# Two-layer hybrid decoder trunk: whole rows of the output projection behind the last pair of heads, and an opening of the MLP in a written-out order with two column pairs interleaved

## The chip, the cores and the metric

One core of one Trainium2 chip runs the whole program. The metric is the device time of one execution in microseconds (us). PE is TensorE, DVE is VectorE, ACT is ScalarE, POOL is GpSimd, SP is the engine that issues most of the DMAs.

## The reference, cut to what matters

Sequence 1024, width 1024, 12 mixing heads and 4 memory heads of 64, MLP width 2816, two layers.

```python
for layer in range(2):
    xn = rmsnorm(h, norm_mix[layer])
    heads = concat(mixer(xn), memory_attention(xn, mem))      # layer 0 FoX, layer 1 dilated
    h = h + merge_heads(heads) @ w_out[layer]                 # the output projection
    u = rmsnorm(h, norm_ffn[layer]) @ w_up[layer]             # 1024 -> 5632
    val, gate = split(causal_depthwise_conv3(u))
    h = h + (silu(gate) * val) @ w_down[layer]
return rmsnorm(h, norm_final)
```

## The kernel before, in words

**Number format.** Every float32 operand of a large product is split into a rounded high part and a low part, and each product is made of three matmuls: high·high, high·low, low·high (`mm3g`, L172, the matmuls on L177 to L179). A weight block is loaded by `load_w` (L107): DMA into `wraw`, cast to `whi` on ACT (L122), subtraction to `wlo` on POOL (L123). There are three `whi`/`wlo` pairs and four `wraw` buffers.

**Layout.** Activations are feature-major: eight blocks of 128 features, two halves of 512 positions. Heads are worked two at a time in six pairs. The attention loop (L808) runs 96 steps: step s issues the scores of block s, the transposes of block s-2 (L495, copied out by ACT on L496 and DVE on L497) and, for odd blocks, the product with the values of block s-3 (L800). `fold` (L499) adds the two halves of such a product and, for the last pair, writes its high and low part straight into the operand tile (L508, L509). An object `Fill` puts chunks of other PE work between these pieces, paced by a cost and a due step given to each item.

**Output projection.** A row n (128 features of h) needs eight chunks of 128 head features. Chunk 5 belongs to the last pair and is ready last. `out_part(half)` (L567) makes seven of the eight chunks for all eight rows as fill work and adds them to the residual (L582): for half 0 due by step 94, for half 1 due by step 104, so that part of half 1 is left to `fill.drain` behind the loop. `out_final` (L300) then adds the eighth chunk of all eight rows from one weight block `wol`, with the residual on L293 and the squares for the norm on L154 to L158. For half 0 it runs inside the loop at step 94, for half 1 at the start of the MLP (L1001). `norm_stages` (L134) turns the squares into a scale: a column sum on PE (L138), DVE, a power on POOL (L142), a diagonal on DVE (L144), a broadcast on PE (L148).

**MLP up-projection.** 22 column pairs j. Each is made by seven products (a Strassen-like scheme) of 4 chunks x 3 matmuls from seven operand sets TS[0] to TS[6], which are sums and differences of quarters of the normalised h. `up_x0` (L351) makes sets 0 and 1 from half 0, `up_x1` (L360) makes sets 2 to 6 from half 1: normalisation on DVE (L348), sum on DVE or POOL (L342), cast on ACT (L343), low part on DVE or POOL (L344). The weight sums of a pair come from `w_alpha` to `w_gamma` (L880 to L909), with casts on L912 and low parts on L915, from raw loads on L870. Products of one pair are combined in PSUM on DVE (L943 to L961), then convolved (`conv_a` on ACT, L971; two `conv_d` on DVE, L975), gated (L979, L983) and stored.

**What sets the order.** In attention and at the start of the MLP only PE follows the order of the code; ACT, DVE, POOL and the DMA queue are ordered by the tile scheduler. From pair 2 on (L1039) PE, ACT, DVE and POOL all follow the order of the code. Pairs 0 and 1 are made before that, largely product by product (L1004 to L1034): the products wait for `up_x1`, and pair 2 waits for PSUM banks that the convolutions of pairs 1 and 0 still read.

```python
run(out_final(l, 1, acc, lambda n: bank_of("all", ALL)))   # L1001
...
product(1, 4, 4)
up_x1(l, rb)                                               # L1012
for j, b in ((0, 0), (1, 4)):
    u21(j)
    product(j, 3, b + 1)
```

Of the kernel before, what the change touches and what calls it, by code (L numbers as in the profile page):

```python
# [29 lines left out]
def trunk(ctx, tc, a, out):  # L30
# [76 lines left out]
    def load_w(src, cols=1024):  # L107
        hi = sb.tile([P, 1024], R32, tag="whi", name="whi", bufs=3)
        lo = sb.tile([P, 1024], R32, tag="wlo", name="wlo", bufs=3)
# [190 lines left out]
    def out_final(l, half, acc, psum):  # L300
        oh, ol = O[l, half]
        c = NPAIR - 1
        hi, lo = load_w(a["wol"][l])
        for n in range(KD):
            ps = psum(n)
            mm3(ps, lambda k: cols(hi)(n), lambda k: cols(lo)(n), lambda k: oh[:, c, :], lambda k: ol[:, c, :], 1)
            residual(ps, n, half, PART[l] if half else None)
            nc.sync.dma_start(hf_scr[l][n][half], H[half](n))
            square_acc(acc, H[half](n), n == 0)
            yield n  # L310
# [6 lines left out]
    def t_tile(i):  # L317
        if i < 4:
            t = sb.tile([P, 2, 4, HT], R32, tag=("xh0", "xl0", "xh1", "xl1")[i], name=f"t{i}")
            TS[i] = lambda x, c: t[:, x, 2 * c:2 * c + 2, :]  # L320
        else:
            us = []
            for u in range(4):
                v = 4 * (i - 4) + u
                us.append((qk(f"t{i}") if v < 10 else ptt(f"t{i}", [P, T])).rearrange("p (k t) -> p k t", k=2))
            TS[i] = lambda x, c: us[2 * x + c]
        return TS[i]
# [7 lines left out]
    def t_make(i, c, a0, a1, op, e0, e1):  # L335

        t = TS[i] if i in TS else t_tile(i)
        hi, lo = t(0, c), t(1, c)
        src = a0
        if a1 is not None:  # L340
            src = (a1 if i == 5 else a0) if i > 4 else qk("tsum", F32).rearrange("p (k t) -> p k t", k=2)
            e0.tensor_tensor(src, a0, a1, op=op)  # L342
        nc.scalar.copy(hi, src)  # L343
        e1.tensor_tensor(lo, src, hi.bitcast(F32), op=ALU.subtract)  # L344
# [6 lines left out]
    def up_x0(l, rb):  # L351
        TS.clear()
        V, G = nc.vector, nc.gpsimd
        norm_in_place(l, 0, rb, range(KD))
        for c in range(2):
            t_make(0, c, quarter(0, 0, c), None, None, None, (V, G)[c])
        for c in range(2):
            t_make(1, c, quarter(1, 0, c), quarter(0, 0, c), ALU.subtract, (V, G)[c], (V, V)[c])

    def up_x1(l, rb):  # L360
        V, G = nc.vector, nc.gpsimd
        q = quarter
        norm_in_place(l, 1, rb, (0, 1, 4, 5, 2, 3, 6, 7))
        for c in range(2):
            t_make(2, c, q(0, 1, c), q(1, 1, c), ALU.subtract, V, (V, G)[c])
        for c in range(2):
            t_make(3, c, q(1, 1, c), None, None, None, (G, V)[c])
        for c in range(2):
            t_make(4, c, q(0, 0, c), q(1, 1, c), ALU.add, (V, G)[c], (V, V)[c])
        for c in range(2):  # L370
            t_make(5, c, q(0, 0, c), q(0, 1, c), ALU.add, (V, G)[c], V)
        for c in range(2):
            t_make(6, c, q(1, 0, c), q(1, 1, c), ALU.add, (V, G)[c], V)


    def attention_phase(l):
        with tc.manual_schedule(engines={mybir.EngineType.PE}):
# [189 lines left out]
            def out_part(half):  # L567
# [4 lines left out]
                else:  # L572
                    hp = [qk("hp", F32).rearrange("p (n t) -> p n t", n=2) for _ in range(4)]
                    dst = PART[l] = lambda n: hp[n // 2][:, n % 2, :]
                for n in range(KD):
                    load_h(l, n, half, dst)
                for n in range(KD):
# [7 lines left out]
            def out_last():  # L585
                acc = sqt("acc")
                for n in out_final(l, 0, acc, lambda n: psp()):
                    yield 648
                g = norm_stages(acc, psp)
                while True:  # L590
                    yield None
                    rb = next(g)
                    if rb is not None:
                        break
                up_x0(l, rb)
# [127 lines left out]
            QK, V, OP = 24 * 216, 96 * 113, 168 * 216  # L723
# [32 lines left out]
            fill.add(out_part(0), OP, 94, 83, "o0")  # L756
            fill.add(out_part(1), OP, 104, 84, "o1")
# [50 lines left out]
            for s in range(len(seq) + D + 1):  # L808
# [9 lines left out]
                if b % 2 == 1:  # L818
# [5 lines left out]
                    if s == LAST:  # L824
                        fill.need("o0")
                        while next(last, None) is not None:
                            fill.step()
# [5 lines left out]
                if s in (LAST + 2, LAST + 3):  # L833
                    next(last, None)
                fill.go(0.30 if b % 2 == 1 else 0.50)
            fill.drain()


# [4 lines left out]
    def ffn(l):  # L843
# [9 lines left out]
        sets = itertools.cycle("wpwpw")  # L853
        two = lambda t: t.rearrange("p (q n) -> p q n", q=2)

        def w_set():
            if next(sets) == "w":
                return (two(sb.tile([P, 1024], R32, tag="whi", name="ahi", bufs=3)),
                        two(sb.tile([P, 1024], R32, tag="wlo", name="alo", bufs=3)))
            return two(ptt("ahi", [P, 1024])), two(ptt("alo", [P, 1024]))  # L860
# [56 lines left out]
        def prep(j):  # L917
            w_raw(j)
            for f, eng in ((w_alpha, G), (w_beta, G), (w_delta, V), (w_gamma, G)):
# [76 lines left out]


        prep(0)
        h_tiles(1)
        acc = sqt("acc")  # L1000
        run(out_final(l, 1, acc, lambda n: bank_of("all", ALL)))  # L1001
        prep(1)
        st = norm_stages(acc, lambda: bank_of("norm", (3, 7)))
        product(0, 2, 2)  # L1004
        s_copy(0, 2)
        next(st)
        product(1, 2, 6)
        s_copy(1, 2)
        product(0, 4, 0)
        rb = next(st)  # L1010
        product(1, 4, 4)
        up_x1(l, rb)  # L1012
        for j, b in ((0, 0), (1, 4)):
            u21(j)
            product(j, 3, b + 1)
            s_copy(j, 3)
            s_diff(j)
        for j, b in ((0, 0), (1, 4)):
            product(j, 5, b + 3)
            u12(j)  # L1020
        for j, b in ((0, 0), (1, 4)):
            product(j, 1, b + 2)
            s_e(j)
            g_1(j)
            g_2(j)
        w_raw(2)
        for j, b in ((1, 4), (0, 0)):
            product(j, 6, b + 1)
            u22(j)
        for j, b in ((0, 0), (1, 4)):  # L1030
            product(j, 7, b + 2)
            u11(j)
        whole(1, 4)
        whole(0, 0)  # L1034
        for f in (w_alpha, w_beta, w_delta, w_gamma):
            o = f(2)
            cast(o)
            rest(o, G)
        with tc.manual_schedule(engines={mybir.EngineType.PE, mybir.EngineType.Activation, mybir.EngineType.DVE,  # L1039
                                         mybir.EngineType.Pool}):  # L1040
            one = itertools.cycle((4, 5, 6, 7))
            for j in range(2, FFC):
                k = j + 1
                more, back = k < FFC, j > 2
# [3 lines left out]
                if back:  # L1048
                    u11(j - 1)
                    conv_a(j - 1, 0, 0)  # L1050
                    conv_d(j - 1, 1, 1)
                s_copy(j, 2)
                product(j, 3, next(one))
                if back:
                    conv_d(j - 1, 1, 2)
                    silu(j - 1)
                    conv_d(j - 1, 0, 1)
# [3 lines left out]
                if back:  # L1061
                    conv_d(j - 1, 0, 2)
# [230 lines left out]
```

## Time and profile before

| | us |
|---|---|
| median of 3 runs | 2657.45 (2651.96 to 2662.17) |
| profiled execution, its own time | 2654.48 |
| its span | 2652.7 |
| PE busy in it | 2453.4 (92%) |
| mean granted clock of PE | 0.969 of full |

Each busy time is a share of the span; a busy PE is not always a PE at full clock, so the granted clock of a stretch is read beside it. What an engine waited for stands in brackets behind an instruction of the timeline: the idle time just before it, and the instruction that ended the wait.

### The profile page before, as it was taken

The page shows a single profiled execution, that of the slowest core. Times are in us where ns is not written, and L with a number is a line of the kernel's source. Part 1 is how long each engine was busy: PE and PEld are TensorE (multiplying, and loading weights), DVE is VectorE, ACT ScalarE, POOL GpSimd, SP SyncE. Part 2 cuts the span into 40 slices and gives each one's busy share as a digit, 9 for nine tenths or more (in the row PEclk, how much of TensorE's full clock was granted, in tenths as well). Part 3 has the DMA queues.
Part 4 walks back from the last instruction along what each step waited for, and adds up shares of the span by engine and source line. Part 5 has one row for each costly group of instructions (what it writes and reads, how often), then busy time and mean ns, then how long its engine had stood idle before and what let it go on. Part 6 is the DMA issues. An engine that isn't in the chain of part 4 may idle for free. (4 is left out here: it accounts for less than half of the span.)

```text
span 2652.7 us, 34480 instructions
## 1 busy us (share of the span) xinstructions
PE 2453.4 (92%) x12280; PEld 2044.6 (77%) x12280; DVE 1645.2 (62%) x2824; ACT 1204.8 (45%) x2189; POOL 1232.9 (46%) x764
## 2 busy tenths in 40 slices
PE   4989999987799999999998999989878999999998
PEld 3868888776588888888877888877657888887886
DVE  5667676666866666633347777775777666666322
ACT  4545555543343444443345555564434343444321
POOL 4201101344667666555543333335545667665542
PEclk9999999998899999999999999999989999999999
DMA  5122222431222222654432222244212222237432
GB/s 179 46 77 73 61 68 88 145 123 64 76 83 88 76 92 73 227 186 138 151 118 63 61 59 70 61 119 146 99 48 97 87 79 88 77 120 234 147 121 79
DMA packets 144980, 271.15 MB, mean 102 GB/s; under 512 B 18844, under 2 KB 23580, under 8 KB 144808
## 3 DMA queue, kind: packets, MB, share of 16 engines
q1 hardware_dynamic: 143944, 268.26, 31.4%
q8 instruction: 96, 1.57, 0.3%
q10 hardware_dynamic: 864, 0.69, 0.1%
q14 instruction: 76, 0.62, 0.1%
HBM read 200.67 MB, written 47.24 MB: 93 GB/s over the span
## 5 line engine op out<-in xcount | busy, mean ns | idle before, releaser
L123 POOL TENSOR_TENSOR wlo<-wraw,whi 128x512 fp32r<-128x512 f32 x354 | 468.6, 1344 | 788.0 <-ACT whi L122 693.6
L177 PE MATMUL PS<-t,ahi 128*128 128x512 f32 x1056 | 418.7, 396 | 34.7 <-ACT t L343 11.4
L178 PE MATMUL PS<-t,ahi 128*128 128x512 f32 x1056 | 416.1, 394 | 11.7 <-DVE t L344 11.7
L179 PE MATMUL PS<-t,alo 128*128 128x512 f32 x1056 | 415.7, 394 | 0.0
L177 PE MATMUL PS<-xh,whi 128*128 128x512 f32 x704 | 311.9, 443 | 29.9 <-DVE hp L582 9.6
L122 ACT CAST whi<-wraw 128x512 fp32r<-128x512 f32 x354 | 202.8, 607 | 223.9 <-issue 65.1
L178 PE MATMUL PS<-xl,whi 128*128 128x512 f32 x704 | 289.5, 411 | 9.1 <-POOL xl L289 4.5
L179 PE MATMUL PS<-xh,wlo 128*128 128x512 f32 x704 | 288.0, 409 | 4.3 <-POOL wlo L123 4.3
L177 PEld LDWEIGHTS PS<-t,ahi 128*128 128x128 f32 x1056 | 201.4, 191 | 81.5 <-issue 17.0
L971 ACT ACTIVATE cv<-PS,cw 128x1024 f32<-128x1024 f32 x88 | 106.2, 1209 | 318.6 <-DVE PS L952 311.2
L178 PEld LDWEIGHTS PS<-t,ahi 128*128 128x128 f32 x1056 | 201.4, 191 | 54.8 <-DVE t L344 12.7
L179 PEld LDWEIGHTS PS<-t,alo 128*128 128x128 f32 x1056 | 201.1, 190 | 42.5
L975 DVE SCALAR_TENSOR_TENSOR cv<-PS,cw,cv 128x1023 f32<-128x1023 f32 (+1 forms) x176 | 221.0, 1277 | 12.7 <-ACT cv L971 10.0
L915 POOL TENSOR_TENSOR alo<-araw,ahi 128x1024 fp32r<-128x1024 f32 x84 | 204.6, 2435 | 33.2 <-ACT ahi L912 33.2
L486 ACT ACTIVATE y<-y,m 128x128 f32<-128x128 f32 (+1 forms) x192 | 149.4, 778 | 117.2 <-DVE m L482 115.2
L497 DVE TENSOR_TENSOR ptl<-PS,pth 128x512 fp32r<-128x512 f32 (+3 forms) x288 | 152.4, 550 | 62.4 <-ACT pth L496 61.5
L177 PEld LDWEIGHTS PS<-xh,whi 128*128 128x128 f32 x704 | 140.4, 199 | 59.3 <-ACT xh L288 10.3
L496 ACT CAST pth<-PS 128x512 fp32r<-128x512 f32 (+3 forms) x288 | 131.2, 479 | 114.9 <-PE PS L495 113.4
L179 PEld LDWEIGHTS PS<-xh,wlo 128*128 128x128 f32 x704 | 139.4, 198 | 36.2 <-POOL wlo L123 5.2
L178 PEld LDWEIGHTS PS<-xl,whi 128*128 128x128 f32 x704 | 140.2, 199 | 32.3 <-POOL xl L289 7.8
L1106 DVE TENSOR_TENSOR g<-graw,g 128x512 fp32r<-128x512 f32 x88 | 90.8, 1063 | 107.7 <-ACT g L1105 107.7
L495 PE MATMUL PS<-ident,y 128*128 128x128 f32 x864 | 130.5, 278 | 28.3 <-DVE ptl L497 28.1
(202 smaller groups left out, 5764.6 us busy)
## 6 DMA issues: line engine op xcount, KB each, us to landing
araw<-in_wu SPq DMA_DIRECT2D x176, 256.0 KB, 3.6
wraw<-in_wd SPq DMA_DIRECT2D x168, 256.0 KB, 3.1
gscr<-cv SPq DMA_DIRECT2D x44, 512.0 KB, 2.6
graw<-gscr SPq DMA_DIRECT2D x88, 256.0 KB, 3.9
wraw<-in_wo SPq DMA_DIRECT2D x64, 256.0 KB, 3.0
wraw<-in_wq SPq DMA_DIRECT2D x56, 256.0 KB, 2.9
hfscr<-h SPq DMA_DIRECT2D x32, 256.0 KB, 2.1
h<-hfscr SPq DMA_DIRECT2D x32, 256.0 KB, 3.7
```

The costliest lines, as they stand in the source:

```text
L122: nc.scalar.copy(hi[:, w], raw[:, :n])
L123: nc.gpsimd.tensor_tensor(lo[:, w], raw[:, :n], hi[:, w].bitcast(F32), op=ALU.subtract)
L177: nc.tensor.matmul(ps, lhsT=whi(k), rhs=xhi(k), start=(first and k == 0), stop=False)
L178: nc.tensor.matmul(ps, lhsT=whi(k), rhs=xlo(k), start=False, stop=False)
L179: nc.tensor.matmul(ps, lhsT=wlo(k), rhs=xhi(k), start=False, stop=(last and k == nk - 1))
L486: nc.scalar.activation(y[:, :nk], y[:, :nk], AF.Exp, bias=m[:, npc - 1:npc], scale=-1.0, accum_out=m[:, 2:3])
L495: nc.tensor.transpose(tp[:, jj, :], y[:, j * P:(j + 1) * P], ident)
L496: nc.scalar.copy(ph, tp[:, :nj, :])
L497: nc.vector.tensor_tensor(pl, tp[:, :nj, :], ph.bitcast(F32), op=ALU.subtract)
L915: eng.tensor_tensor(o[2], o[0], o[1].bitcast(F32), op=ALU.subtract)
L971: nc.scalar.activation(t, u, AF.Identity, bias=w(3), scale=w(2))
L975: V.scalar_tensor_tensor(t[:, d:], u[:, :T - d], w(2 - d), t[:, d:], op0=ALU.mult, op1=ALU.add)
```

## The change: what it does

For half 0, `out_part` makes six partial rows in place of eight; rows 6 and 7 are made whole, with eight chunks, by the new `out_rest`, which also adds the last chunk to rows 0 to 5. For half 1 there are four partial rows, due by step 98 in place of 104, and four whole ones. The order of the whole rows ("c") and last chunks ("f") is written out, over the three score banks (half 0) or four banks (half 1). In the loop, steps 94 to 98 each take a few of them. The sum of squares runs one row late. `up_x0` and the new order of `up_x1` have all sums and low parts on DVE. The weights of the pairs alternate between the `pt` and `qk` buffers, operand sets 5 and 6 move into the `whi`, `wlo` and `tab` buffers, and the down-projection's weights move to `pt`. Pairs 0 and 1 have each product twice in a row, one for each pair, their combination is regrouped (`s_less`, `g_0`), and pair 2's products alternate with the convolutions of pairs 1 and 0. PE, ACT, DVE and POOL all follow the code's order from the half-1 rows on.

```diff
-    def load_w(src, cols=1024):
-        hi = sb.tile([P, 1024], R32, tag="whi", name="whi", bufs=3)
+    def load_w(src, cols=1024, home=None):
+        hi = home("whi", [P, 1024]) if home else sb.tile([P, 1024], R32, tag="whi", name="whi", bufs=3)
...
-    def out_final(l, half, acc, psum):
+    def out_rest(l, half, acc, psum, order):
...
+        for i, (kind, n) in enumerate(order):
+            if kind == "f":
+                wl = wl or load_w(a["wol"][l])
+                hi, lo, ks = *wl, [(NPAIR - 1, n)]
+            else:
+                hi, lo, ks = *load_w(a["wo"][l, n]), [(c, c) for c in KORD]
+            ps = psum()
...
+            residual(ps, n, half, PART[l] if half and kind == "f" else None)
             nc.sync.dma_start(hf_scr[l][n][half], H[half](n))
+            sq = acc if i == 0 else sqt("sq")
+            nc.scalar.activation(sq, H[half](n), AF.Square)
+            if late is not None:
+                nc.vector.tensor_tensor(acc, acc, late, op=ALU.add)
...
+    def t_rest(i, c):
+        nc.vector.tensor_tensor(TS[i](1, c), SUM[i, c], TS[i](0, c).bitcast(F32), op=ALU.subtract)
...
-            fill.add(out_part(0), OP, 94, 83, "o0")
-            fill.add(out_part(1), OP, 104, 84, "o1")
+            fill.add(out_part(0, 6), 6 * OP, 94, 83, "o0")
+            fill.add(out_part(1, 4), 4 * OP, 98, 84, "o1")
...
+                order = [("c", 6)] + [("f", n) for n in range(6)] + [("c", 7)]
...
-        sets = itertools.cycle("wpwpw")
+        sets = itertools.cycle([ptt] * 3 + [qk_set] * 3)
...
+        for j in range(2):
+            w_raw(j)
+            prep(j, (w_alpha, w_beta, w_delta, w_gamma)[:4 - j], G)
...
+        with tc.manual_schedule(engines=engines):
+            acc = sqt("acc")
+            run(out_rest(l, 1, acc, lambda: bank_of("fin", (0, 1, 2, 3)),
+                         [("c", 4), ("f", 0), ("f", 1), ("c", 5), ("f", 2), ("f", 3), ("c", 6), ("c", 7)]))
+            prep(1, (w_gamma,), G)
+            product(0, 2, 6)
+            s_copy(0, 2)
+            st = norm_stages(acc, lambda: bank_of("norm", (7, 5)))
+            next(st)
+            product(1, 2, 2)
+            s_copy(1, 2)
+            product(0, 4, 0)
+            rb = next(st)
+            product(1, 4, 4)
+            u21(0)
+            for c in range(2):
+                norm_in_place(l, 1, rb, (4 + 2 * c, 5 + 2 * c))
+                SUM[3, c] = q(1, 1, c)
+                t_cast(3, c)
+            t_rest(3, 0)
...
+            product(0, 5, 3)
+            product(1, 5, 7)
+            product(0, 3, 1)
+            s_copy(0, 3)
+            s_less(0)
+            product(1, 3, 6)
+            s_copy(1, 3)
+            s_less(1)
+            for c in range(2):
+                t_sum(4, c, q(0, 0, c), q(1, 1, c), ALU.add)
+                t_cast(4, c)
...
+            product(1, 7, 6)
+            product(0, 7, 2)
+            w_raw(2)
+            u22(1)
+            conv_a(1, 1, 4)
+            prep(2, (w_alpha, w_beta), G)
...
+            product(2, 2, 4)
...
+            product(2, 1, 6)
+            u22(0)
+            conv_a(0, 1, 0)
...
-                hi, lo = load_w(a["wd"][l, b0 + b])
+                hi, lo = load_w(a["wd"][l, b0 + b], home=ptt)
```

## Rows read from the trace of the kernel before

**Rows 1.** The page: span and busy time of each engine.

```profile
span 2652.7 us, 34480 instructions
PE 2453.4 (92%) x12280; PEld 2044.6 (77%) x12280; DVE 1645.2 (62%) x2824; ACT 1204.8 (45%) x2189; POOL 1232.9 (46%) x764
```

**Rows 2.** Windows: span, busy PE, PEld, DVE, ACT, POOL (instructions), granted clock, DMA.

```profile
563.10:646.00 82.90, 64.44 (x268) 48.73 (x268) 60.07 (x78) 33.96 (x55) 38.95 (x22) 0.91 0.27 96
646.00:724.20 78.20, 59.58 (x227) 46.40 (x227) 64.21 (x57) 29.28 (x32) 40.61 (x17) 0.85 0.19 64
1815.00:1861.50 46.50, 45.95 (x248) 39.17 (x247) 28.26 (x70) 25.59 (x54) 26.60 (x20) 1.00 0.36 114
1860.90:1943.50 82.60, 63.92 (x268) 48.62 (x267) 59.74 (x77) 33.88 (x53) 38.94 (x22) 0.91 0.28 97
1943.50:2021.45 77.95, 59.13 (x227) 46.01 (x227) 64.16 (x57) 29.23 (x32) 41.16 (x17) 0.86 0.18 64
2040.00:2080.00 40.00, 40.00 (x178) 33.12 (x177) 26.52 (x32) 16.20 (x18) 27.07 (x14) 1.00 0.24 88
```

**Rows 3.** Timeline of PE, layer 1, projection: start, us, [idle before <-releaser].

```profile
1863.05 0.49 PE L177 MATMUL PS<-xh,whi 128*128 128x512 f32 x1 [2.10 <-ACT xh L508]
1872.41 0.51 PE L177 MATMUL PS<-xh,whi 128*128 128x512 f32 x1 [0.39 <-DVE h L293]
1884.08 1.54 PE L495 MATMUL PS<-ident,y 128*128 128x128 f32 x6 [2.10 <-DVE ptl L497]
1917.41 0.47 PE L177 MATMUL PS<-xh,whi 128*128 128x512 f32 x1 [2.78 <-DVE hp L582]
1932.38 0.80 PE L179 MATMUL PS<-xh,wlo 128*128 128x512 f32 x1 [2.32 <-POOL wlo L123]
1943.50 0.80 PE L177 MATMUL PS<-t,ahi 128*128 128x512 f32 x1 [4.53 <-DVE h L293]
```

**Rows 4.** Timeline of PE, layer 1, opening of the MLP.

```profile
1964.70 0.80 PE L177 MATMUL PS<-t,ahi 128*128 128x512 f32 x1 [5.72 <-ACT t L343]
1971.34 0.80 PE L178 MATMUL PS<-t,ahi 128*128 128x512 f32 x1 [5.84 <-DVE t L344]
2007.34 0.77 PE L177 MATMUL PS<-t,ahi 128*128 128x512 f32 x1 [4.10 <-DVE cv L975]
```

**Rows 5.** Timeline of DVE, layer 1, around the last product with the values.

```profile
1892.16 2.87 DVE L144 TENSOR_TENSOR dg<-ident,nrs 128x512 f32<-128x512 f32 x1
1898.46 5.34 DVE L348 SCALAR_TENSOR_TENSOR h<-h,gains,PS 128x512 f32<-128x512 f32 x8
1908.08 0.69 DVE L505 TENSOR_TENSOR fold<-PS,fold 64x512 f32<-64x512 f32 x1
1914.91 1.64 DVE L509 TENSOR_TENSOR xl<-fold,xh 64x512 fp32r<-64x512 f32 x1
```

**Rows 6.** Lines L344 and L342: duration ns min/median/max.

```profile
L344 DVE TENSOR_TENSOR t<-tsum,t x10: 1209/1226/3357, 613.6 to 1981.8; 128x1024 fp32r<-128x1024 f32 x10
L342 DVE TENSOR_TENSOR tsum<-h,h x8: 2036/2838/3381, 607.9 to 1971.2; 128x1024 f32<-128x1024 f32 x8
L343 ACT CAST t<-tsum x12: 1043/1045/1057, 612.5 to 1976.9; 128x1024 fp32r<-128x1024 f32 x12
```

**Rows 7.** Timeline of POOL and ACT, layer 1.

```profile
1910.26 1.30 POOL L123 TENSOR_TENSOR wlo<-wraw,whi 128x512 fp32r<-128x512 f32 x1
1917.65 2.37 POOL L915 TENSOR_TENSOR alo<-asum,ahi 128x1024 fp32r<-128x1024 f32 x1
2014.44 0.59 ACT L935 COPY s<-PS 128x512 f32<-128x512 f32 x1 [2.08 <-PE PS L179]
2016.99 1.21 ACT L971 ACTIVATE cv<-PS,cw 128x1024 f32<-128x1024 f32 x1 [1.01 <-POOL cv L983]
```

**Rows 8.** Groups by line, DVE, two pairs of the steady loop (2060 to 2098 us).

```profile
L975 DVE SCALAR_TENSOR_TENSOR cv<-PS,cw,cv 128x1023 f32<-128x1023 f32 (+1 forms) x8 | 10.1, 1278 | 0.1
L884 DVE TENSOR_TENSOR asum<-araw 128x1024 f32<-128x1024 f32 x2 | 2.4, 1216 | 0.0
L946 DVE TENSOR_TENSOR PS<-PS,s 128x512 f32<-128x512 f32 x3 | 2.1, 700 | 6.1 <-PE PS L179 6.1
```

More of the change, by code (lines that the diff above doesn't have):

```diff
@@ L564, in mem_attn, with out_part @@
                     fill.go(.3)
-            def out_part(half):
+            def out_part(half, rows):
                 oh, ol = load_o(l, half)
@@ L586, in out_last @@
                 acc = sqt("acc")
[L587 to L592, printed above, removed]
+                order = [("c", 6)] + [("f", n) for n in range(6)] + [("c", 7)]
+                yield from out_rest(l, 0, acc, lambda: bank_of("fin", (0, 1, 2)), order)
+                for rb in norm_stages(acc, psp):
                     if rb is not None:
-                        break
-                up_x0(l, rb)
+                        up_x0(l, rb)
+                    yield
             def forget():
@@ L825, in attention_phase @@
                         fill.need("o0")
-                        while next(last, None) is not None:
-                            fill.step()
+                        next(last)
+                    elif s == LAST + 2:
+                        for _ in range(4):
+                            next(last)
+                    elif s == LAST + 4:
+                        next(last)
                     fill.go(.1)
@@ L832, in attention_phase, with qk_set @@
                     emit_t(s - D)
-                if s in (LAST + 2, LAST + 3):
-                    next(last, None)
+                if s == LAST + 1:
+                    for _ in range(3):
+                        next(last)
+                elif s == LAST + 3:
+                    next(last)
                 fill.go(0.30 if b % 2 == 1 else 0.50)
             fill.drain()
+    def qk_set(name, shape):
+        return qk(name)
     def ffn_phase(l):
@@ L852, in ffn @@
         A, R = {}, {}
-        sets = itertools.cycle("wpwpw")
+        sets = itertools.cycle([ptt] * 3 + [qk_set] * 3)
         two = lambda t: t.rearrange("p (q n) -> p q n", q=2)
         def w_set():
[L857 to L860, printed above, removed]
+            home = next(sets)
+            return two(home("ahi", [P, 1024])), two(home("alo", [P, 1024]))
         def w_raw(j):
@@ L1018, in ffn @@
[L1018 to L1038, printed above, removed]
@@ L1041, in ffn @@
             one = itertools.cycle((4, 5, 6, 7))
-            for j in range(2, FFC):
+            for j in range(3, FFC):
                 k = j + 1
-                more, back = k < FFC, j > 2
+                more = k < FFC
                 if more:
@@ L1116, in g1_tile @@
             two = lambda t: t.rearrange("p (x t) -> p x t", x=2)
-            return two(qk("g1") if k < 18 else ptt("g1", [P, T]))
+            if k < 18:
+                return two(qk("g1"))
+            return two(sb.tile([P, T], R32, tag=("whi", "wlo")[k % 2], name="g1", bufs=3))
         G1 = []
```

213 lines of the change are left out of this document (131 added, 82 removed).

## The prediction

> **What bounds the kernel now.** The page comes first: PE is busy 92% of the span and no other engine reaches two thirds [rows 1]. So time can come only from PE's idle 200 us and from the stretches in which it works at the lower of its two clocks, 1.2 instead of 2.4 GHz. Next, a table of the span in windows shows where these lie. In the steady loop of the up-projection PE is busy 40.00 of 40 us at full clock, 178 matmuls, so 0.225 us each [rows 2]. The change touches two stretches per layer. Stretch A goes from the end of the product that frees half 0 to the first MLP product; stretch B goes on to the point where pair 2 is three products in and PE runs without gaps. In layer 1, A has 82.60 - 63.92 = 18.7 us idle, and a granted clock of 0.91 over 82.6 us costs at most 0.09 x 82.6 = 7.4 us: 26 us. B has 18.8 us idle and 0.14 x 78 = 10.9 us from the clock: 30 us. Layer 0 gives 26 and 30 as well [rows 2]. That is 56 us per layer, **112 us in all, the whole pool.**
>
> Then the timeline of PE, read for its brackets, says what ended each wait. In A: the high part of the last pair's output (2.10), the residual of a last chunk (0.39, seven times alike or longer), transposes behind DVE (2.10), partial rows behind DVE (2.78), a late low part of the weights (2.32), and the bank of the last row (4.53) [rows 3]. In B: operand sets 2 and 3, of which PE waits first for a cast, then for a low part (5.72, 5.84), and a convolution that holds a bank (4.10) [rows 4]. After most of these gaps matmuls start to start take about twice as long for a few us; that is the clock's part.
>
> **The change, part by part.** The matmuls are the same in number, only their order differs, and so are the loads on SP: 16 row blocks and two last-chunk blocks per layer. So everything below is waiting.
>
> *Pace of the fill.* Ten partial rows over 14 steps (0.67 row per step by the code's arithmetic) replace a pace of 0.76. PE was busy 45.95 of 46.50 us there [rows 2]; with 0.09 x 21 x 0.225 = 0.4 us less work per step, PE either goes faster or idles 0.4 us. Bounds 0 and 4 us per layer; I take 0, since PE was the full engine.
>
> *Half 0 (steps 94 to 98).* A whole row of 24 matmuls (5.4 us) with the last pair's chunk at its end now stands where PE waited 2.10 us, so the fold is covered; three banks and other work between the last chunks remove the 0.39s. What is late next: the score banks are shared with the rows, 0.5 us (0 to 2, at most two such DVE passes). The last transposes come right before the last values product; PE waited 2.10 us for such a copy before; I take 1 (0 to 2.1). The scale needs POOL and a DVE diagonal that took 2.87 us beside POOL [rows 5]; PE has some 3 us of work meanwhile; 0.5 (0 to 2.9).
>
> *Half 1.* The first whole row now starts right behind the last values product. Its seven earlier chunks last 21 x 0.225 = 4.7 us; the fold's two DVE steps spanned 8.5 us before (1908.08 to 1916.55) because normalisation stood between them [rows 5]. The fold is now issued ahead of normalisation, so I take 1 (0 to 4). The weights' low parts on POOL, 1.30 each [rows 7], two per row, go beside six pair splits of 2.37; PE waited 2.32 once before; 1.5 (0 to 5). **DVE is what is late next.** Behind the last values product it has the fold (1.4), eight normalisations (5.34), six operations of 1024 columns at 1.21, and some 3 us of weight sums [rows 5, 6, 8]: 17 us before it adds the first whole row to the residual. PE wants that row's bank again after 0.5 + 5.4 + 1.4 + 5.4 = 12.7 us. So 5 us (0 if DVE gets to the residual between, 11 if its operations stretch as far as the 3.36 us rows). Clock loss behind these waits: 4 (2 to 7.4). Sum for A: 0.5 + 1 + 0.5 + 1 + 1.5 + 5 + 4 = 13.5 us, bounds 6 to 24 since not all happen together.
>
> *Opening (B).* I walk the written order with a product as 2.7 us, normalisation 0.67, cast 1.05, sum and low part 1.21, PSUM combination 0.61 to 0.70, convolution 1.21 and 1.28 [rows 5 to 8], zero at the norm's scale. No sum of two quarters ran below 2.04 us [rows 6], since POOL was always at work beside it; the same shape took 1.22 as a weight sum [rows 8], and here POOL has only one 512-column subtraction per pair, so I take 1.21 (up to 3.38).
> - Product (1,4) ends at 2.7. Set 3's second low part waits for six normalisations, a combination and two low parts: 7.1. Products on set 3 end 2.8 us late.
> - Set 2 is complete at 13.9; wait 2.2.
> - Set 4: its first cast stands on ACT behind the copy of product (1,3) (0.59) [rows 7], which ends at 18.5; its second low part is ready at 25.2, behind one sum for set 5; wait 5.5, the largest.
> - Sets 5 and 6 are then in time.
> - PE ends these products at 40.3. Pair 2's products wait for convolutions in banks 4 to 7 and 0 to 3, with the raw weights of pair 2 landing just before: 1.6 + 3.0 + 1.1 + 2.6.
>
> Sum 18.8 us of waits; clock behind the three larger ones 5 (2 to 10): 24 us, bounds 17 to 35. The gaps of 5.72, 5.84 and 4.10 shrink to one of 5.5 and several below 3. What hides the rest is the other pair's product, 2.7 us each; without it each wait would be longer by that.
>
> *Weights and down-projection buffers.* Six sets in place of five, three pairs for the down weights as before: 0, hidden by a PE that is full there [rows 2]; the price if this fails is the fourth rival.
>
> **Sum.** Per layer (26 - 13.5) + (30 - 24) = 18.5 us, twice 37. The profiled execution took 2654.5 (span 2652.7), 3.0 below the median of 2657.45. So 2617.5 for such an execution and **2620 for the median.**
>
> **Rivals.**
> - *The waits all but close*: DVE takes residuals between its other work, casts come earlier than my walk has them. A 7, B 18: 2 x (19 + 12) = 62, 2595. For: every wait of rows 3 and 4 is addressed by a reordering. Against: DVE was already busy 64 of 78 us in B [rows 2].
> - *DVE takes PE's place.* All sums and low parts move from DVE and POOL to DVE. The low parts took 1.21 us at least and 3.36 at most [rows 6], the long ones beside POOL. At 1.8 us each my walk gives 28.7 us of waits, 35 with the clock, and A 18.5: 2 x (7.5 - 5) = 5 us gained, 2652. For: POOL has 20 us of splits behind the last values product. Against: in the opening POOL is nearly empty. The Trainium skill, page "SBUF — State Buffer", section "Who interferes with whom", speaks against this change: a DVE instruction with two SBUF inputs and a GpSimd instruction that reads SBUF use one shared read interface, and the one that is issued second is blocked until the first ends. By that rule A comes out as in this rival and B as in my walk, 2 x (7.5 + 6) = 27 us gained, 2630; the spread of rows 6 agrees with it.
> - *The change doesn't do what it says*: POOL gets the splits of pairs 0 and 1 ahead of the first whole row's weights. Those splits wait for buffers that the last values product still reads and for raw loads that wait for the first splits: 1 + 6 us of POOL, 5 us of loading, then 5 us of casts and sums and 7 us of POOL, two low parts: the first whole row starts some 26 us late. A 34 with DVE's backlog gone: 2 x (-8 + 6), 2661. Against: the same kind of splits was interleaved with weights before, one of each within 8 us [rows 7].
> - *Slower: the steady loop loses its cover.* Sets 5 and 6 sit in the `whi`, `wlo` and two of three `tab` buffers, so the next pair's weight sum has one buffer, and DVE stands still in its written order if that is not free. Price: 38 pairs; from 1 us per pair the change is lost, at 1.5 us it is 2620 + 57 = 2677. Against: sum, cast and low part take 1.2 + 1.05 + 2.4 = 4.7 us of a pair's 84 x 0.225 = 18.9 [rows 2, 6 to 8]; it decides only if they end 14 us later than that.
>
> **How the numbers follow.** Forecast 0.59, waits closed 0.15, DVE 0.12, POOL's order 0.06, steady loop 0.08. A measurement of this kernel can tell about 0.5%, 13 us, from no change. Faster by more: 0.59 + 0.15 = 0.74; within: 0.12 + 0.06 = 0.18; slower: 0.08. The bounds of A and B put the forecast's own case at 2600 to 2643; the range reaches to 2586, which takes in most of the closed case, and to 2655, which takes in the DVE case, and leaves out POOL's order, the steady loop and the tail below, under 0.2.
>
> **What would show it.** Right: in A no brackets behind the last pair's high part nor runs of 0.39 behind residuals, the granted clock of A and B above 0.93, a bracket of about 5 us behind DVE at the fifth or sixth piece of half 1, and one in the opening at set 4. Wrong: brackets over 2 us behind `wlo` at the first whole row (POOL's order), DVE without idle time through B with low parts over 1.8 us (DVE's case), or any PE gap per pair in the steady loop.

## The result, and the profile after

The kernel after takes **2687.56 us** (median, 2681.34 to 2691.83) beside 2654.70 for the kernel before: ratio **1.0118, interval 1.0085 to 1.0151**. It is slower by 1.2%, where 2620 was forecast. The profiled execution took 2691.83, the longest of its four, with a span of 2689.8. One execution in the experiments below, of the early operand alone on the kernel after, took 4091.9 us at a granted clock of 0.556 and is left out of its median.

The page, span and busy engines, beside [rows 1]:

```profile
span 2689.8 us, 34462 instructions
PE 2465.0 (92%) x12280; PEld 2044.5 (76%) x12280; DVE 1605.5 (60%) x2822; ACT 1206.6 (45%) x2189; POOL 1186.6 (44%) x754
```

PE's work is the same. The windows (columns as in [rows 2]) show where it stands: the end of attention, the rows of half 1 in layers 0 and 1, and the steady loop.

```profile
540.00:565.00 25.00, 20.14 (x98) 15.06 (x97) 11.27 (x30) 12.50 (x25) 15.81 (x13) 1.00 0.39 128
565.00:600.00 35.00, 34.73 (x185) 29.17 (x184) 23.39 (x40) 15.80 (x29) 11.75 (x8) 1.00 0.27 98
600.00:640.00 40.00, 16.68 (x41) 10.45 (x41) 27.00 (x24) 15.00 (x21) 22.83 (x12) 0.63 0.32 107
1920.00:1960.00 40.00, 19.17 (x49) 13.10 (x50) 26.40 (x24) 13.45 (x18) 19.79 (x11) 0.62 0.33 112
2080.00:2120.00 40.00, 40.00 (x178) 33.14 (x177) 27.14 (x33) 17.15 (x19) 25.17 (x12) 1.00 0.22 79
```

The first two windows of the kernel before:

```profile
540.00:565.00 25.00, 23.08 (x125) 19.19 (x123) 13.97 (x33) 14.05 (x29) 17.57 (x13) 1.00 0.45 147
565.00:600.00 35.00, 29.04 (x124) 21.12 (x125) 26.13 (x38) 15.29 (x28) 14.25 (x10) 0.90 0.31 110
```

In layer 0, half 0 behind the last pair went as planned: 34.73 of 35 us busy, against 29.04. Layer 1 kept one wait there, for the bank of a row whose residual was late:

```profile
1900.43 0.79 PE L177 MATMUL PS<-xh,whi 128*128 128x512 f32 x1 [2.10 <-DVE h L293]
```

Before half 0's rows 3 us are lost, and then comes the loss itself: of the 40 us behind the last product with the values PE works 17 to 19, at 0.62 to 0.63 of full clock. The timeline of PE says for what, from 600 us on, beside [rows 3]; layer 1 has the same six waits, each within 0.3 us:

```profile
611.26 0.80 PE L177 MATMUL PS<-xh,whi 128*128 128x512 f32 x1 [10.39 <-ACT whi L122]
629.20 0.79 PE L177 MATMUL PS<-xh,whi 128*128 128x512 f32 x1 [9.29 <-ACT whi L122]
631.83 0.79 PE L179 MATMUL PS<-xh,wlo 128*128 128x512 f32 x1 [1.41 <-POOL wlo L123]
635.85 0.80 PE L177 MATMUL PS<-xh,whi 128*128 128x512 f32 x1 [1.95 <-ACT whi L122]
648.56 0.80 PE L177 MATMUL PS<-xh,whi 128*128 128x512 f32 x1 [3.05 <-ACT whi L122]
659.32 0.50 PE L177 MATMUL PS<-xh,whi 128*128 128x512 f32 x1 [2.01 <-ACT whi L122]
```

In half 1 nothing of [rows 3] is left; in its place PE waits mostly for **casts of weights**. The queues show why each cast is late. First SP's issues:

```profile
596.49 9.08 SPq L879 DMA_DIRECT2D araw<-in_wu  x4
605.62 0.90 SPq L121 DMA_DIRECT2D wraw<-in_wo  x2
```

The first whole row's weights are issued behind four loads for pair 1 (L879), whose buffers POOL frees (SP waits 11.8 us for POOL's low parts there); their cast follows 5 us later. Then ACT:

```profile
610.59 1.13 ACT L122 CAST whi<-wraw 128x512 fp32r<-128x512 f32 x2
...
627.06 1.04 ACT L921 CAST ahi<-araw 128x1024 fp32r<-128x1024 f32 x1 [5.77 <-DVE araw L907]
628.01 0.63 ACT L317 ACTIVATE acc<-h 128x512 f32<-128x512 f32 x1
628.54 1.12 ACT L122 CAST whi<-wraw 128x512 fp32r<-128x512 f32 x2
633.38 0.63 ACT L317 ACTIVATE sq<-h 128x512 f32<-128x512 f32 x1 [3.71 <-DVE h L293]
634.66 0.63 ACT L317 ACTIVATE sq<-h 128x512 f32<-128x512 f32 x1 [0.65 <-DVE h L293]
635.20 0.60 ACT L122 CAST whi<-wraw 128x512 fp32r<-128x512 f32 x1
```

The second of these casts, at 628.54, is that of the last-chunk block. The loop of `out_rest` writes each block's cast (L122) behind the square of the row before it (L317). From half 1 on ACT follows the code, so a block is cast only when PE has made the row before, DVE has added it and ACT has squared it: a round trip at each block. The first trip is long because DVE gets to the residual only at 626.95, behind pair 1's weight sums.

In the opening of layer 0 the waits are short, beside [rows 4]:

```profile
681.47 0.50 PE L178 MATMUL PS<-t,ahi 128*128 128x512 f32 x1 [0.87 <-DVE t L360]
691.10 0.50 PE L178 MATMUL PS<-t,ahi 128*128 128x512 f32 x1 [0.76 <-DVE t L360]
696.87 0.49 PE L177 MATMUL PS<-t,adia 128*128 128x512 f32 x1 [1.62 <-ACT t L357]
736.34 0.76 PE L177 MATMUL PS<-t,ahi 128*128 128x512 f32 x1 [2.36 <-DVE cv L983]
```

**The balance by landmarks.** From half 0's first projection matmul to the first MLP product it is 150.3 and 152.1 us before, 169.9 and 173.6 after: 41 lost. From there to the first down-projection matmul it is 448.2 and 447.9 before, 440.6 twice after: 15 gained. The other 11 of the 37 us between the two spans lie thinly, 2 ahead of the first projection, 6 between the layers, 3 at the end; they were not traced to a cause.

### The profile page after: what moved, and what is told of

The parts are those of the page before. It is cut to its first block, busy times and chain, and to the rows that moved or that the text cites. A ratio compares the mean times of both kernels' runs of the same rounds, so it can differ in the third digit from the quotient of the medians.

```text
span 2689.8 us, 34462 instructions
## 1 busy us (share of the span) xinstructions
PE 2465.0 (92%) x12280; PEld 2044.5 (76%) x12280; DVE 1605.5 (60%) x2822; ACT 1206.6 (45%) x2189; POOL 1186.6 (44%) x754
## 5 line engine op out<-in xcount | busy, mean ns | idle before, releaser
L123 POOL TENSOR_TENSOR wlo<-wraw,whi 128x512 fp32r<-128x512 f32 x354 | 462.6, 1327 | 826.3 <-ACT whi L122 712.9
L122 ACT CAST whi<-wraw 128x512 fp32r<-128x512 f32 x354 | 202.9, 607 | 225.5 <-issue 54.7
L924 POOL TENSOR_TENSOR alo<-araw,ahi 128x1024 fp32r<-128x1024 f32 x88 | 212.4, 2414 | 7.8 <-ACT ahi L921 7.8
L178 PEld LDWEIGHTS PS<-xl,whi 128*128 128x128 f32 x704 | 142.3, 202 | 47.4 <-POOL xl L289 21.7
L293 DVE TENSOR_TENSOR h<-h,PS 128x512 f32<-128x512 f32 x56 | 37.7, 684 | 230.2 <-PE PS L1283 141.1
```

What stands on the lines that cost most here:

```text
L122: nc.scalar.copy(hi[:, w], raw[:, :n])
L123: nc.gpsimd.tensor_tensor(lo[:, w], raw[:, :n], hi[:, w].bitcast(F32), op=ALU.subtract)
L178: nc.tensor.matmul(ps, lhsT=whi(k), rhs=xlo(k), start=False, stop=False)
L924: eng.tensor_tensor(o[2], o[0], o[1].bitcast(F32), op=ALU.subtract)
```

## The experiments

All times are medians. The kernel before was measured anew beside each of the four groups of runs (2657.58, 2656.69, 2655.84 and 2654.20), and the ratios are to that. Differences of medians across groups carry up to 3 us of this spread.

### The casts, the loads, the written order

Casts ahead: the weight blocks are loaded and cast ahead of the squares, in the same order as they are used.

```diff
         for i, (kind, n) in enumerate(order):
+            for key in (ahead or {}).get(i, ()):
+                weights(key)
...
-                         [("c", 4), ("f", 0), ...]))
+                         [("c", 4), ("f", 0), ...], ahead={0: (4, "l", 5), 3: (6,), 6: (7,)}))
```

> The changed kernel, with one thing different: in the whole rows of half 1 each weight block is loaded and cast one row earlier in the written order (the first three blocks ahead of the first row, the fourth ahead of the second whole row, the fifth ahead of the third). Theory 'squares': in the written order ACT casts the next row's weights only after the square of the row before, and that waits for PE and DVE. Then the brackets behind the cast and the low part of the weights after the first (9.3, 1.4, 2.0, 3.1, 2.0, 0.6 us in layer 0) fall below 1 us each, some 18 us and 4 us of clock per layer, and the first of 10.4 us stays or changes by less than 4: about 2645. Theory 'loads': the raw loads stand on SP behind pair 1's raw loads and behind stores, so the casts only find another thing to wait for; the brackets keep their sum within 5 us per layer and end on a DMA: 2675 to 2690.

Loads first: the first whole row's block and the last-chunk block are loaded and cast ahead of the splits of pairs 0 and 1.

```diff
+        pre = {k: load_w(a["wol"][l] if k == "l" else a["wo"][l, k]) for k in (4, "l")}
         for j in range(2):
             w_raw(j)
```

> The changed kernel, with the loads and casts of the first whole row's weights and of the last-chunk block of half 1 issued ahead of the splits of pairs 0 and 1; nothing else is moved. Theory 'loads': the first bracket (10.4 us) falls to under 3, the second (9.3 us) stays within 3 us of that or falls with it since its load is ahead too, the later ones (1.4 to 3.1) stay: 10 to 20 us and some clock per layer, 2640 to 2665. Theory 'squares' alone: the first bracket stays, since the first row's cast has no square of this half before it; 2680 to 2690.

Rows unwritten: `out_rest` of half 1 stands outside the block in which ACT, DVE and POOL follow the code.

```diff
+        run(out_rest(l, 1, acc, ...))
         with tc.manual_schedule(engines=engines):
-            run(out_rest(l, 1, acc, ...))
```

> The changed kernel, with the rows of half 1 outside the written order: PE keeps it, but ACT, DVE and POOL are ordered by the scheduler there, as in the kernel before. Theory 'squares': the scheduler puts casts ahead of squares, so the brackets after the first go as in the run with casts ahead, about 2645. Theory 'loads': as with casts ahead, 2675 to 2690. If the whole rows as such were the cost (more row weights behind the last pair), nothing of it changes: 2685.

Measured: casts ahead 2649.42, ratio 0.9971 [0.9959, 0.9982]; rows unwritten 2646.79, 0.9973 [0.9963, 0.9983]; loads first 2673.14, 1.0072 [1.0054, 1.0089]. The first two come out near what the theory of the squares gave; loads first lies between its two theories. PE with the casts ahead:

```profile
611.09 0.79 PE L177 MATMUL PS<-xh,whi 128*128 128x512 f32 x1 [10.40 <-ACT whi L122]
621.76 0.50 PE L177 MATMUL PS<-xh,whi 128*128 128x512 f32 x1 [1.26 <-ACT whi L122]
...
631.37 0.80 PE L179 MATMUL PS<-xh,wlo 128*128 128x512 f32 x1 [4.75 <-POOL wlo L123]
```

PE with the loads first:

```profile
607.54 0.50 PE L177 MATMUL PS<-xh,whi 128*128 128x512 f32 x1 [1.17 <-ACT xh L519]
609.04 0.50 PE L178 MATMUL PS<-xl,whi 128*128 128x512 f32 x1 [1.01 <-DVE xl L520]
625.42 0.79 PE L177 MATMUL PS<-xh,whi 128*128 128x512 f32 x1 [14.27 <-ACT whi L122]
```

The two edits take away different waits. The written order on ACT is worth 38 us: with the casts ahead the 9.29 falls to 1.26 and the waits behind later casts are gone, though a new wait of 4.75 us for a low part on POOL stands in their place. The edit moves a block's load together with its cast. It matters little whether the blocks are written ahead or left to the scheduler. The loads are worth 14 us alone; the 10.4 falls to the fold's 2.2, but the next cast then waits 14.27 behind the square.

Both together:

> Both parts together: the loads of the first whole row and of the last-chunk block are issued ahead of the splits of pairs 0 and 1, and each later block's load and cast is written ahead of the squares before it. Theory (two queues in written order, SP and ACT, each holds the weights back): the wait of 10.4 us at the first whole row shrinks to the fold's 2 us as it did with the loads moved alone, and the waits behind casts at rows 5, 6 and 7 stay gone as they did with the casts moved alone; row 5's load is still behind pair 1's, so up to 5 us may stay there. 2 x 6 us below the 2649 of the casts alone: 2637, between 2630 and 2643, under both the kernel before and every version so far. Rival (DVE's residuals, my prediction's 5 us, are next in line and take over): gaps behind 'DVE h' of 5 us or more appear in the rows, and the time stays at 2645 to 2650. Rival (the two parts cover the same wait): 2649, no further gain.

> The first two loads ahead of the splits, and the rows of half 1 outside the written order, so that the scheduler places their casts, squares, residuals and low parts. Theory: the same as loads and casts together, 2636 (2628 to 2642); the 10.4 us at the first whole row falls to 2 to 3 us. Rival (the scheduler puts the pair splits' casts ahead of row 5's whatever the loads' order): a gap of 8 to 14 us behind ACT whi at row 5, and 2646.

Measured: **2637.63**, 0.9928 [0.9913, 0.9943]; unwritten 2640.15, 0.9943 [0.9927, 0.9960]. Both times lie in the expected ranges. But the wait that the rival named is there too, 9.81 us with loads and casts together and 13.04 with the rows unwritten. PE with loads and casts together:

```profile
627.15 0.80 PE L177 MATMUL PS<-xh,whi 128*128 128x512 f32 x1 [9.81 <-DVE h L293]
```

It stands at the fifth piece, where the first row's bank is wanted again. DVE in the same run:

```profile
620.93 5.57 DVE L914 TENSOR_TENSOR araw<-araw 128x512 f32<-128x512 f32 x2
626.42 0.67 DVE L293 TENSOR_TENSOR h<-h,PS 128x512 f32<-128x512 f32 x1
```

Pair 1 behind the rows: in the code all its loads, casts and splits, with the casts ahead.

```diff
-        for j in range(2):
-            w_raw(j)
-            prep(j, (w_alpha, w_beta, w_delta, w_gamma)[:4 - j], G)
+        w_raw(0)
+        prep(0, (w_alpha, w_beta, w_delta, w_gamma), G)
...
-            prep(1, (w_gamma,), G)
+            w_raw(1)
+            prep(1, (w_alpha, w_beta, w_delta, w_gamma), G)
```

> Casts written ahead, and all loads and splits of pair 1 behind the rows of half 1, so that neither SP, ACT nor POOL has pair 1's work ahead of the rows' weights. Theory (it is pair 1's loads and splits that hold up the first whole row, 10.4 us, and wo5's low part, 4.75 us): both waits fall below 3 us; the product of pair 1 then waits for its own weights, some 3 us once. 2649 - 2 x (7 + 3 - 3): 2635, between 2627 and 2645. Rival (pair 0's splits, or the buffers that the last product with the values frees, hold it): the 10.4 stays, and 2645 to 2652.

Measured 2646.97, 0.9970 [0.9958, 0.9981]: the rival's range. But SP does not follow the code's order, and on its queue three of pair 1's four loads still stand ahead of the first row's weights (pair 0's went out before 530 us):

```profile
594.80 8.62 SPq L886 DMA_DIRECT2D araw<-in_wu  x3
603.48 0.90 SPq L121 DMA_DIRECT2D wraw<-in_wo  x2
```

The weights are issued 2.14 us earlier than in the kernel after, and PE's first wait is 8.28 us, shorter by 2.11. So the run does not clear pair 1's loads, although its time lies in the rival's range. What it moved are the casts and splits, and with them the 4.75 for a low part fell to 1.62. The first MLP product comes 4 us sooner than with loads and casts, at 638.39, and the opening takes 447 to 449 us in place of 440, since pair 1's weights are now late.

### The opening alone

The old projection in front of the new opening, then the same with one low part and one sum of operand sets 0 and 1 on POOL, as before the change.

```diff
-            t_rest(0, c)
+            (V, G)[c].tensor_tensor(TS[0](1, c), SUM[0, c], ...)
```

> The kernel before with the new opening of the MLP alone (operand sets on DVE, products of two pairs interleaved, new homes of the weights), and the old output projection: eight partial rows per half and the old last chunks. From the first MLP product to the first down-projection matmul the changed kernel took 440.6 us, the kernel before 448.2. If the opening's gain is its own: 7.5 us per layer, 2640. If it owes to the late start (weights of pairs 0 and 1 ready while PE waited in the rows), that stretch stays near 448 and the time at 2650 to 2660.

> The old projection with the new opening, as in the opening alone (2660), but half of operand sets 0 and 1 back on POOL as in the kernel before. Theory (sets 0 and 1 wholly on DVE delayed the partial rows of half 1, the gaps of 8.27 and 4.07 us behind 'DVE hp'): those gaps fall to 2.8 and 2.3 as before, first MLP product at 646, and the opening keeps its gain of 7 us per layer: 2657 - 14 = 2643 (2639 to 2648). Rival (the gaps come from the weights' buffers or the residuals' order, not from DVE's share): gaps of 8 and 4 us stay, 2656 to 2662.

Measured 2660.00, 1.0011 [0.9998, 1.0023], and **2643.52**, 0.9957 [0.9943, 0.9971]. From the first MLP product to the first down-projection matmul the first takes 440.1 and 444.2 us, the second 439.8 and 439.9: the opening's gain is its own, up to 8 us per layer. What had spoilt it in the first was the missing share on POOL, ahead of the MLP. Behind DVE's partial rows PE waited 8.27 and 4.07 us there, and in the second, less than before but more than the 2.8 and 2.3 expected,

```profile
622.97 0.76 PE L177 MATMUL PS<-xh,whi 128*128 128x512 f32 x1 [5.10 <-DVE hp L575]
637.94 0.76 PE L177 MATMUL PS<-xh,whi 128*128 128x512 f32 x1 [3.36 <-DVE hp L575]
```

### DVE's queue: POOL share, banks, the third weight sum

The same POOL share, now with loads and casts together; six banks in place of four for the rows of half 1; both; and half 1's operand loaded earlier beside both.

```diff
-            run(out_rest(l, 1, acc, lambda: bank_of("fin", (0, 1, 2, 3)),
+            run(out_rest(l, 1, acc, lambda: bank_of("fin", (0, 1, 2, 3, 4, 5)),
...
                 for n in range(rows):
+                    if half == 0 and n == 2:
+                        load_o(l, 1)
```

> Loads and casts together, and half of operand sets 0 and 1 back on POOL (one low part and one sum, 1.2 to 1.9 us each on DVE). In loads and casts together PE's largest wait was 9.81 us behind DVE's residual of the first whole row, and DVE worked through 20 us of normalisations, sets 0 and 1 and weight sums before it. Theory (DVE's queue sets this wait): it shrinks by what is taken off DVE, 2.4 to 3.1 us, per layer: 2637.6 - 5 to 6: 2632 (2628 to 2635). Rival (POOL, now with two operations of 1024 columns more, is late with row 5's low part, or they stretch DVE's own through the shared reads): no gain, 2636 to 2643.

> Loads and casts together, with six PSUM banks in place of four for the rows of half 1. PE's wait of 9.81 us was for a bank that DVE's late residual still reads. Theory (only the bank passes DVE's lateness on to PE): PE runs two more pieces before it needs a bank again, 5.4 + 1.4 = 6.8 us, so the 9.81 shrinks to 3 or less: 2637.6 - 2 x 6.5: 2625 (2620 to 2630). Rival (DVE remains the longest chain up to the column sum): the bracket reappears as a wait of 7 us or more behind DVE acc or h before the scale, and 2634 to 2638.

> Loads and casts, six banks, and the POOL share together. If the bank and DVE's queue are two parts of one wait, what the banks leave (about 3 us) goes with DVE's 2.5: 2620 (2614 to 2627). If six banks alone already leave no wait, the same as six banks, 2625; if POOL is late in place of DVE, 2630.

> The same as banks and POOL together, with half 1's operand loaded during row 2 of half 0 instead of at the first partial row of half 1. Five waits behind ACT xh and POOL xl, 3.5 to 4.9 us per layer, stood there in the kernel after, and none in the kernel before. Theory (the shorter first item of the fill lets PE reach this load before it has landed): they go: 2 x 3.5 to 2 x 4.9 below the run with banks and POOL, by about 8 us. Rival (the fill's pace gives the time back later, since the loop's own work then waits for its chain): no difference of over 3 us.

Measured: POOL share 2647.65, 0.9963 [0.9949, 0.9977]; six banks 2641.52, 0.9940 [0.9925, 0.9955]; both 2649.00, 0.9969 [0.9955, 0.9984]; with the early operand 2638.57, 0.9929 [0.9911, 0.9948]. The first three miss, all upwards. With the POOL share, POOL:

```profile
612.60 2.36 POOL L381 TENSOR_TENSOR t<-h,t 128x1024 fp32r<-128x1024 f32 x1 [3.48 <-ACT t L364]
614.93 4.46 POOL L123 TENSOR_TENSOR wlo<-wraw,whi 128x512 fp32r<-128x512 f32 x2
```

The share on POOL that gained 16 us in the old projection costs 10 here: the whole rows' low parts on POOL now stand behind it, and PE waits 3.39 us for one and still 7.62 for DVE. With six banks, ACT:

```profile
623.71 1.04 ACT L928 CAST ahi<-araw 128x1024 fp32r<-128x1024 f32 x1 [5.78 <-DVE araw L914]
624.67 0.63 ACT L324 ACTIVATE acc<-h 128x512 f32<-128x512 f32 x1
625.20 1.13 ACT L324 ACTIVATE sq<-h 128x512 f32<-128x512 f32 x2
626.24 1.12 ACT L122 CAST whi<-wraw 128x512 fp32r<-128x512 f32 x2
```

PE's wait there is 10.79 us, behind this last cast: the bank is free, but row 6's cast stands behind squares that wait for the same late residual. It is one chain, DVE's queue, and it reaches PE by the bank or by the cast. The early operand is worth 10.4 us in this pair.

To test DVE's queue itself, pair 1's third weight sum was written behind the sixth piece:

```diff
-            prep(j, (w_alpha, w_beta, w_delta, w_gamma)[:4 - j], G)
+            prep(j, (w_alpha, w_beta, w_delta, w_gamma)[:4 - 2 * j], G)
...
+            for _ in range(6):
+                next(rows)
+            prep(1, (w_delta,), G)
```

> Loads and casts together, and half 1's operand loaded during row 2 of half 0. Theory (the operand load is a cost of its own, 10.4 us in the pair of runs with banks and POOL, and does not hang on the rest): 2637.6 - 8 to 10: 2628 (2625 to 2632), no gap behind POOL xl. Rival (its gain there came with the other waits, and DVE's queue takes it back here): 2634 to 2638.

> The run before it, and pair 1's third weight sum (two DVE operations, 5.57 us in all beside POOL, ahead of the first residual) written behind the sixth piece of half 1, where DVE waited for PE. Theory (DVE's queue ahead of the first residual sets PE's wait of 9.8 us): the wait falls by 5 to 6 us per layer, to about 4: 2628 - 10: 2617 (2613 to 2622). Rival (POOL's splits, not DVE, hold the rows, or the sum costs as much where it now stands): 2625 to 2630.

> The kernel after with this one edit: half 1's operand loaded during row 2 of half 0. The five gaps behind ACT xh and POOL xl, 4.9 us per layer, go. Theory (ACT's and DVE's order behind the rows is counted from the end of attention, so nothing waits for it): 2687.6 - 2 x 4.9: 2678 (2674 to 2682). Rival (the loads and splits behind set the time of the first row, not PE): the gap of 10.4 us at the first whole row grows by what is gained, and 2684 to 2690.

> Early operand, loads and casts, the third weight sum behind the sixth piece, and six banks. In six banks alone, the wait stood behind ACT whi of row 6, whose cast is written behind three squares that wait for DVE's residuals. Theory (one chain, DVE's queue, reaches PE by the bank or by the cast, whichever is first): with DVE earlier by 5.6 us, either way the same wait is left: within 4 us of the run with four banks, 2617. Rival (with DVE earlier, four banks are the next limit): 5 us or more faster than with four.

Measured: early operand on loads and casts 2633.56, 0.9919 [0.9900, 0.9938]; with the sum moved **2627.28, 0.9906 [0.9886, 0.9925]**, ahead of both the kernel before and the kernel after; six banks beside it 2628.99, 0.9905 [0.9890, 0.9921]; the early operand alone on the kernel after 2681.11 (three executions), 1.0107 [1.0086, 1.0128], which its interval does not tell from the kernel after. By medians the early operand gains 4 us on loads and casts, where 8 to 10 were expected, and the sum 6 more, where 10 were; the first stops just short of its rival's range, the second lies in its rival's, and the intervals overlap, so neither size is shown by the times. The traces show the waits: half 1's operand is waited for no more, and alone on the kernel after the first whole row's wait stays at 10.40, against the rival; the sum's move shortened the wait behind DVE as foretold.

PE, early operand on loads and casts:

```profile
622.27 0.79 PE L177 MATMUL PS<-xh,whi 128*128 128x512 f32 x1 [9.80 <-DVE h L293]
```

PE, with the sum moved:

```profile
616.92 0.80 PE L177 MATMUL PS<-xh,whi 128*128 128x512 f32 x1 [4.30 <-DVE h L293]
623.00 0.80 PE L179 MATMUL PS<-xh,wlo 128*128 128x512 f32 x1 [2.30 <-POOL wlo L123]
```

PE is back 5.35 us earlier, yet the first MLP product starts only 1.1 us earlier (636.4 against 637.5). The windows with the sum moved show where the rest went:

```profile
618.00:622.00 4.00, 2.70 (x7) 1.56 (x5) 3.90 (x5) 2.31 (x5) 4.00 (x3) 0.50 0.69 266
622.00:626.00 4.00, 3.00 (x7) 2.44 (x8) 4.00 (x6) 1.26 (x2) 2.64 (x2) 0.50 0.42 125
626.00:630.00 4.00, 4.00 (x18) 3.21 (x17) 0.47 (x2) 2.19 (x3) 2.45 (x2) 0.95 0.53 137
```

The same two windows without the move:

```profile
618.00:622.00 4.00, 0.00 (x0) 0.00 (x0) 4.00 (x3) 0.34 (x1) 3.08 (x2) 0.50 0.00 0
622.00:626.00 4.00, 3.73 (x8) 2.32 (x8) 3.63 (x5) 3.30 (x6) 3.22 (x2) 0.52 0.52 197
```

Of the 4.25 us that are lost again, 2.3 are waits for low parts on POOL, 2.30 and 0.90 us in place of 0.88, since pair 1's splits still stand ahead of them there. That much of the rival holds. Most of the rest is the clock: it had fallen to the lower level, 0.50, during the wait, and 15 matmuls start about 0.43 us apart where without the move 8 do. Layer 1 agrees: its wait falls from 9.76 to 4.31, and 1.2 us of that are left at the first MLP product. Six banks beside it are the same within the intervals, as the one chain would have it.

## Why the prediction was wrong, point by point

**The pool and the opening: right.** B was to gain 6 us per layer; it gained 7.6 and 7.3, and 8 with the old projection in front. What is left above 22 pairs of 84 matmuls at 0.225 us is 440.6 - 415.8 = 24.8 us, forecast 24; the same count gives 32.4 for the kernel before, where the prediction had 30, so some 2 us of it lie outside B. The waits were shorter than walked (set 4's 5.5 came out as 1.62 + 0.99 + 0.20 + 0.46; pair 2's products waited 5.9 in place of 8.3), so the total is right with more of it in slow or other work than I had. The low parts there took 1.22 us but for one of 1.45, as taken: in B DVE did not take PE's place. In A, beside POOL, two low parts took 1.49 and 2.29 and the two operations of a weight sum 2.8 us each, so the rival's stretch is real there, and of its two versions the one with the stretch in A alone fits.

**Half 0: right.** Of the 2 us foreseen for banks, transposes and scale, 0.3 us were seen in layer 0 and 2.1 in layer 1. There a residual stood behind a weight sum (1.77 us) and an accumulation (1.75 us) that DVE made beside POOL, against 0.68 each in layer 0.

**The fill's pace: mis-sized.** I took 0, with bounds 0 and 4. Five waits of 0.28 to 1.49 us for half 1's operand, 4.9 us in all with ACT's, stand at 547 to 559 us of the kernel after, because the shorter first item brings PE to that load sooner. Loading it earlier took these waits away. By medians that gave 10 us in one pair of runs, clear of the noise, and 4 and 6 in two others that are not.

**The failing step** is the one on half 1's weights: "The weights' low parts on POOL, 1.30 each [rows 7], two per row, go beside six pair splits of 2.37; PE waited 2.32 once before; 1.5 (0 to 5)", with, above it, "so are the loads on SP". The waits behind these weights, the last-chunk block's included, came to 28.7 us in layer 0, and the clock's loss with them. I counted the loads and casts of a block and gave them POOL's price; where they stand on SP's and ACT's queues I did not walk, though I walked the written order of the opening, and the same block makes ACT follow the code here. The runs put it in numbers: ACT's order 38 us, SP's order 14, both 50, of the 67 between forecast and result.

**The fold: mis-sized by 1 us.** 1 us, bounds 0 to 4; with the loads first it shows as 1.17 + 1.01. The reason given for its 8.5 us before is misread: normalisation had ended at 1903.80 [rows 5], and what stood between the two DVE steps were two low parts of set 1, 3.47 us from 1911.41.

**DVE is late next: right in kind, short in size.** 5 us, bounds 0 to 11, at the fifth piece: with loads and casts in time the wait is there, at the fifth piece, and measures 9.8. From the fold to the residual DVE took 21.7 us (604.77 to 626.42 with loads and casts) in place of 17, since pair 1's third weight sum alone took 5.57 beside POOL where the sum had 3 for all weight sums. In the kernel after the same lateness reached PE sooner, by ACT's square and cast, where I had no route for it. Without DVE's third sum it is 4.3.

**The rivals.** POOL's order came nearest: pair splits do stand ahead of the first row's weights, and 2661 had the right sign against the forecast, but it had the row 26 us late once, with nothing behind it; here it is 10 us, and then the round trips. The steady loop keeps its cover, 40.00 of 40 us busy. The waits do not all close: the best version found, 2627, is 7 us short of the forecast's 2620, with the order of the queues mended and two terms of its sum paid.

**Clock: mis-sized.** 4 us per layer, bounds 2 to 7.4, for A. From 600 us to the first MLP product at 667.38 PE worked 38.25 us on 110 instructions; at 0.225 us each that is 24.8, so the clock, granted at 0.70 there, took some 13 us, above the bound. The waits that it follows were longer than forecast.

## What to carry to other kernels

Where engines follow the order of the code, walk each queue of the stage, DMA issues too, and ask of every operand's load and cast what stands ahead of it and whom that waits for: a cast written behind a row's reduction turns a prefetch into a round trip. After a wait is gone, look for the same lateness on another route before adding banks or moving work to the engine that looks idle. A move that pays in one order (one low part and one sum on POOL, 16 us) can cost in another (10 us), so it is priced in the queue in which it will stand. And after moving a load in the code, read the DMA queue of the new trace: where a scheduler orders that queue, the load may not have moved.

## What the runs showed of the hardware that was not expected

The third weight sum is two DVE operations of 512 columns with both inputs in SBUF. Beside POOL's splits they took 5.57 us; the same two, moved to where POOL stood idle, took this (DVE, the sum moved):

```profile
625.11 1.28 DVE L916 TENSOR_TENSOR araw<-araw 128x512 f32<-128x512 f32 x2
```

That is 2.82 us each against 0.68. Beside POOL each ended some 0.55 us behind a POOL split that had begun before it (these ended at 623.21 and 625.94). The residuals, with one input in PSUM, took 0.67 to 0.69 us beside POOL and without it. The Trainium skill, page "SBUF — State Buffer", section "Who interferes with whom", has both: a DVE instruction with two SBUF inputs contends with GpSimd's reads, one with at most one, outside the two-port modes, does not; the trace agrees, and puts the stretch at about four times.

And a wait cut from 9.80 to 4.30 us gave PE back only 1.1 of 5.4 us in that stage. About half of the rest went into new waits for POOL; the other part went because the granted clock was at its lower level, 0.50, from 618 us to near 626 in either case, and PE then made at half speed what it had stood still for.
